# A hybrid attention, convolution and expert layer on one core: u blocks between the queries, pacing by VectorE time, gate writes on another queue, and attention values in column halves

## The chip, the cores and the metric

The kernel runs on one core of a Trainium2 chip. The metric is the device time of one execution in microseconds; less is better. Before the change the median of three runs was 1781.04 us (1773.59 to 1781.09).

The engines go by short names in the profile: PE is TensorE (matrix products; PEld is its loading of weights), DVE is VectorE, ACT is ScalarE, POOL is GpSimd, and SP is SyncE, which only issues transfers. SPq and ACTq are the instruction queues of SyncE and ScalarE where they issue a transfer or wait.

## The reference

One layer of a streaming encoder over 512 tokens of width 1024, in float32. What matters here:

- A projection of the normed input gives queries, keys and values of eight heads, an index branch that selects 128 keys per query, a convolution branch and gates. Attention and convolution are mixed by the gates, projected by w_out, and added to x.
- Then a mixture of 16,384 single-neuron experts. Each token has eight heads; each head scores 128 row keys and 128 column keys, takes the 16 best of both, and the 16 best of their sums. That selects 128 experts per token, with a softmax gate per head. In the reference:

```
u = expert_u[et]
v = expert_v[et]
act = jax.nn.gelu(jnp.einsum('tnd,td->tn', u, xt)) * gt
return jnp.einsum('tn,tnd->td', act, v)
```

- A last gated embedding closes the layer.

## The kernel before, in words

The tokens lie in four tiles of 128. The four tiles' experts are worked out in two different ways.

**Tile 0, gathered.** For its 128 tokens the selected rows of peer_u and peer_v are fetched one expert slot at a time by an indirect transfer (line 799), 128 for u and 128 for v. For each, VectorE runs one operation over 128 x 1024 elements (a dot product, L812, or a weighted sum, L814). With eight Gelu steps this makes 264 steps of the generator `gathered` (L777). `tick` (L827) takes `us / TICK` steps of it; the constants QTICK, RTICK, WTICK, RATE_UV and RATE_V say how many are taken in each phase.

**Tiles 1 to 3, dense.** For these 384 tokens all 16,384 experts are computed, in 128 blocks of 128 experts. A u block (`u_prep` L959, `u_step` L968) loads 128 x 1024 of u (`ut`), splits it into a high part `uh` (ScalarE, L964) and a remainder `ul` (VectorE, L965), multiplies (24 matmuls of 128 x 384, L972 to L974) into a PSUM bank `tp` and applies Gelu on ScalarE into `sg` (L975). There are two `tp` banks. A v block multiplies the gated result with 128 rows of v (L1055 to L1061).

The gates of the dense part must stand in a table G_d in DRAM, by expert block and token, before the first v block. They are made by `gates_dense` (L904), tile by tile: `select` (L704) finds the 16 best of the candidate sums and their expert numbers on VectorE, with two small operations on ScalarE (an Exp, L732, and a copy, L744); three transposes on TensorE (L910) turn the result; then, for each of four parts of 32 tokens, one-hot matrices `ohj`, `ohi` and products `og` are made on VectorE (L930 to L933, 128 x 2048 elements each), TensorE multiplies them (`scatter` L942, L948 and L949), ScalarE copies to `stg` (L951), and ScalarE's queue issues four writes of 512 KB to G_d (L956) when a part is complete.

**The phases.** The order is as follows. The times are rough, read from the trace.

1. Up to about 300 us: input projections, index, convolution and attention for tile 0's queries (`attention` L583, `softmax` L536, `weigh` L562).
2. 300 to 400: attention of tiles 1 to 3 is worked in behind `branches`, `residual` and `query` of tile 0.
3. 400 to 500: `branches` (L619) and `residual` (L641) of tiles 1 to 3. Between the four products of `branches`, steps of `sel0` (the selection for tile 0) are taken.
4. 500 to 590: `query` (L833) of tiles 1 to 3. Each of four rounds multiplies by 512 columns of w_peer_q (`prod_T`, with splits `whi` L161 and `wlo` L162), copies the result (`qT`, L839), and runs `rank` (L689) on each tile: scores on TensorE (L692) and, on VectorE, the 16 best of each of four key sets.
5. 590 to 940: the loop of WARM = 64 u blocks (L990). With it runs the generator `work`: all of `gates_dense`, 58 steps. WPACE = 0.9 steps are taken per block, whatever their length. Each pair of u blocks writes its `sg` to DRAM.
6. 940 to 1440: 64 rounds, each with a u block and a v block, and gather steps at RATE_UV.
7. To the end: the v blocks of the first 64, gather steps at RATE_V, and the closing embedding.

**What sets the order.** The Python code says what depends on what. Within an engine the framework puts instructions in an order planned beforehand: earlier lines of the program come first where their operands are expected to be there, later ones fill in. `tc.high_priority()` moves instructions ahead (each u block's preparation two blocks ahead, for instance); `tc.issue_after` keeps one behind another. At run time every engine takes its instructions strictly in that order. A tile pool with `bufs=n` gives n buffers; whoever takes the next one waits for the last reader of that buffer.

Of the kernel before, what the change touches and what calls it, by code (L numbers as in the profile page):

```python
# [34 lines left out]
WPACE = 0.9  # L35
WTICK = 0.5
QTICK = 25.0
# [5 lines left out]
RATE_UV = 0.36  # L43
RATE_V = 0.147
# [24 lines left out]
def layer_kernel(ctx: ExitStack, tc: tile.TileContext, a, out):  # L69
# [31 lines left out]
    def f(t):  # L101
        return t.bitcast(F32)
# [10 lines left out]
    class Stream:  # L113
# [19 lines left out]
        def nat_T(self, pieces, K, x):  # L133
            M = sum(p[2] for p in pieces) // P
            ps = [mm()[:, :x.shape[-1]] for _ in range(M)]
# [426 lines left out]
    def weigh(ap_, top, qt, pr_, L):  # L562
# [11 lines left out]
        av = tp()[:, :2 * P]  # L574
        for kt in range(nk):
            pe.matmul(av, V[:, kt, pr_ * P:(pr_ + 1) * P], PT[:, kt].rearrange("p s q -> p (s q)"),
                      start=(kt == 0), stop=(kt == nk - 1))
# [126 lines left out]
    def select(t, gate, i_out, j_out):  # L704
# [17 lines left out]
        for h in range(H):  # L722
# [9 lines left out]
        act.activation(ex, ex, AF.Exp)  # L732
        sm = sl_.tile([P, H], F32, name="exs", bufs=1)
        v.tensor_reduce(out=sm, in_=ex, axis=AX, op=ALU.add)
        v.reciprocal(sm, sm)
        v.tensor_tensor(out=gate.rearrange("p (k h) -> p h k", h=H), in0=ex,
                        in1=sm.unsqueeze(2).to_broadcast([P, H, 16]), op=ALU.mult)
# [6 lines left out]
        act.activation(dl[:, 0:3:2, 0], sT[:, :, 0], AF.Copy)  # L744
        v.tensor_sub(dl[:, 0:3:2, 1:16], sT[:, :, 1:16], sT[:, :, 0:15])
        mk = sl_.tile([P, 16, P], F16, name="mk", bufs=1)
# [12 lines left out]
        yield  # L759
# [5 lines left out]
        yield  # L765
# [67 lines left out]
    def query(pl, x, xlo, ts, tick=None):  # L833
        for n in range(4):
# [46 lines left out]
    with lpool("y0") as yp:  # L881
        m0 = yp.tile([P, DC, TD], F32R, name="m0")
        m1 = yp.tile([P, DC, TD], F32R, name="m1")
        with lpool("y1") as y1:
            branches(y1, P, TD, m0, m1, lambda us: next(first, None))
        for _ in first:
            pass
        es_0.close()
        with lpool("y2") as y2:
            residual(y2, (1, 2, 3), m0, m1, None, h2_hi, h2_lo, tick, ple)  # L890
    with lpool("qp") as qp:
        query(qp, h2_hi, h2_lo, (1, 2, 3), tick)
# [3 lines left out]

    es_d = ExitStack()
    up = es_d.enter_context(tc.tile_pool(name="up", bufs=1, side="right", reuse_waits="tile"))
# [5 lines left out]
    def gates_dense(t):  # L904
        tt = t - 1
        ijg = gb.tile([P, 3, P], F32, name="ijg", bufs=1)
        yield from select(t, ijg[:, 2], ijg[:, 0], ijg[:, 1])
        p = mm()
# [8 lines left out]
        for part in range(4):  # L917
            stg = gb.tile([P, P // 4, 32, 4], F32, name="stg", bufs=2)
            for t0 in (0, 8):
# [14 lines left out]
                for q0 in (0, 4):  # L934
# [3 lines left out]
                    yield  # L938
# [3 lines left out]
    def scatter(tt, part, t0, q0, stg, ohj, og):  # L942
# [10 lines left out]
        if t0 + q0 == 12:  # L953
            c0 = tt * P + 32 * part
            for b0 in range(0, P // 4, 8):
                act.dma_start(out=G_d[b0:b0 + 8, :, c0:c0 + 32, :].rearrange("b j t f -> j b (t f)"),  # L956
                              in_=stg[:, b0:b0 + 8].rearrange("p b t f -> p b (t f)"))

    def u_prep(i):  # L959
        ut = up.tile([P, DC, P], F32, name="ut", bufs=UTB)  # L960
        sp.dma_start(out=ut, in_=a["uT"][i])
        uh = up.tile([P, DC, P], F32R, name="uh", bufs=UD + 1)
        ul = up.tile([P, DC, P], F32R, name="ul", bufs=UD + 1)
        act.activation(uh, ut, AF.Copy)  # L964
        anchor[0] = v.tensor_sub(ul, ut, f(uh)).ins  # L965
        return uh, ul

    def u_step(uh, ul, sg, s):  # L968
        p = tp()[:, :TD]
        for c in range(DC):  # L970
            xh, xl = h2_hi[:, c, :], h2_lo[:, c, :]
            pe.matmul(p, uh[:, c, :], xh, start=(c == 0), stop=False)  # L972
# [264 lines left out]
```

## Time and profile before

| What | Value |
|---|---|
| Runs | 1781.04, 1781.09, 1773.59 us |
| The profiled execution's own time | 1776.63 us |
| Its span | 1774.9 us |
| ScalarE, GpSimd busy | 661 us, 427 us |
| Transfers | 441.74 MB, 249 GB/s on average |
| G_d writes | 48 of 512 KB, ScalarE's queue |
| Loads of ut and vt | 128 each of 512 KB, SyncE's queue |

How to read the lines of the profile. A group line gives the line of code, engine, operation, what is written and read, shapes and count; then busy time and the mean of one in ns; then the idle time of the engine just before, and what ended it. A wait line says which engine waited at which line for which instruction: total, times, longest. A timeline line begins with the start time and the duration, and ends in brackets with the idle time before it. A line of stretches gives the length, then the busy time of each engine, then the share of TensorE's clock that was granted, the busy share of the transfer engines, and GB/s. Matmuls overlap in the pipeline, and the profile models their ends, so what one costs is read from the distance of two starts. A float32 matmul appears as two records.

### The profile page before, as it was taken

To read this page: it belongs to the slowest core of one execution; us is meant where nothing else is said; L and a number is where in the kernel's file an instruction comes from. 1 tells how busy PE (TensorE), PEld (TensorE's weight loads), DVE (VectorE), ACT (ScalarE), POOL (GpSimd) and SP (SyncE) were. 2 spreads that over 40 slices of the span, in tenths; PEclk is the share of its full clock that TensorE was granted. 3 is DMA by queue.
4 is the path that set the end of the run, shared out by engine and by line. 5 is a ranking of instruction groups with operands and counts; after the bars stand their busy time and mean duration, and the time that the engine had idled before them with its cause. 6 is when DMAs were issued, how large, how long until landed. Compare 5 with 4: busy or idle time off the path is not lost.

```text
span 1774.9 us, 24360 instructions
## 1 busy us (share of the span) xinstructions
PE 1717.2 (97%) x9033; PEld 1487.6 (84%) x9033; DVE 1362.3 (77%) x2489; ACT 660.9 (37%) x981; POOL 427.5 (24%) x301
## 2 busy tenths in 40 slices
PE   6999999999999899999999999999999999999998
PEld 5777677586788888999999999999999988888887
DVE  4889779648769999996857878877877857667763
ACT  3233343340353244444444333333333333334431
POOL 0021000211112113120113645445545511111100
PEclk9999999999999999999999999999999999999999
DMA  5432325756875468788899999899989878888921
GB/s 163 145 120 84 100 84 184 255 174 192 293 266 155 129 227 280 236 273 260 288 293 378 391 329 337 321 340 330 353 306 344 308 260 311 311 291 314 376 87 69
DMA packets 189815, 441.74 MB, mean 249 GB/s; under 512 B 15192, under 2 KB 76888, under 8 KB 189440
## 3 DMA queue, kind: packets, MB, share of 16 engines
q1 hardware_dynamic: 100528, 273.72, 45.1%
q0 software_dynamic: 36864, 134.23, 21.4%
q10 hardware_dynamic: 52304, 32.24, 6.1%
q8 instruction: 71, 1.16, 0.3%
q14 instruction: 48, 0.39, 0.1%
HBM read 391.86 MB, written 52.46 MB: 250 GB/s over the span
## 4 chain that ended last, share of the span: by engine, by line
PE 59%; DVE 7%; issue 4%; DMA 2%; ACT 1%; POOL 0%; SPq 0%; DVEq 0%; ACTq 0%; POOLq 0%
PE tp L972 9%; PE tp L973 9%; PE tp L974 9%; PE mm L1059 6%; PE mm L1060 6%; PE mm L1061 6%; PE at L1060 3%; PE at L1061 3%; PE at L1059 3%; DMA wr<-in_w_ple_gate_dram 1%; PE mm L948 1%; PE mm L949 1%; DVE ul L965 1%; DVE si L702 1%; DVE sc L699 1%
## 5 line engine op out<-in xcount | busy, mean ns | idle before, releaser
L972 PE MATMUL tp<-h_hi,uh 128*128 128x384 f32 x1024 | 350.9, 343 | 11.5 <-ACT sg L975 11.5
L973 PE MATMUL tp<-h_lo,uh 128*128 128x384 f32 x1024 | 347.7, 340 | 0.0
L974 PE MATMUL tp<-h_hi,ul 128*128 128x384 f32 x1024 | 347.4, 339 | 0.0
L799 POOL DMA_INDIRECT grow<-in_peer_u_dram,eidx x128 | 189.0, 1476 | 480.9 <-DVE grow L812 198.2
L799 POOL DMA_INDIRECT grow<-in_peer_v_dram,eidx x128 | 187.3, 1463 | 398.6 <-DVE grow L812 197.9
L1052 DVE TENSOR_TENSOR vl<-vt,vh 128x1024 fp32r<-128x1024 f32 x128 | 156.4, 1222 | 107.7 <-ACT vh L1051 107.5
L964 ACT ACTIVATE uh<-ut 128x1024 fp32r<-128x1024 f32 x128 | 135.5, 1060 | 277.0 <-PE tp L973 252.8
L965 DVE TENSOR_TENSOR ul<-ut,uh 128x1024 fp32r<-128x1024 f32 x128 | 155.8, 1219 | 79.2 <-ACT uh L964 64.4
L972 PEld LDWEIGHTS tp<-h_hi,uh 128*128 128x128 f32 x1024 | 194.7, 190 | 14.6 <-ACT sg L975 13.4
L1051 ACT ACTIVATE vh<-vt 128x1024 fp32r<-128x1024 f32 x128 | 134.9, 1056 | 185.4 <-PE at L1061 138.1
L1059 PE MATMUL mm<-vh,ah 128*128 128x512 f32 x512 | 200.0, 391 | 0.0
L1060 PE MATMUL mm<-vl,ah 128*128 128x512 f32 x512 | 199.2, 389 | 0.3 <-DVE vl L1052 0.3
L1061 PE MATMUL mm<-vh,al 128*128 128x512 f32 x512 | 199.5, 390 | 0.0
L973 PEld LDWEIGHTS tp<-h_lo,uh 128*128 128x128 f32 x1024 | 194.8, 190 | 1.1
L974 PEld LDWEIGHTS tp<-h_hi,ul 128*128 128x128 f32 x1024 | 194.9, 190 | 0.0
L814 DVE SCALAR_TENSOR_TENSOR acc<-grow,gact,acc 128x1024 f32<-128x1024 f32 x128 | 164.3, 1283 | 0.0
L812 DVE SCALAR_TENSOR_TENSOR grow<-grow,h2row 128x1024 f32<-128x1024 f32 x128 | 155.0, 1215 | 5.0 <-DMA grow<-in_peer_u_dram,eidx 5.0
L161 ACT ACTIVATE whi<-wraw 128x1024 fp32r<-128x1024 f32 (+1 forms) x70 | 71.6, 1022 | 178.9 <-PE mm L176 76.5
L162 DVE TENSOR_TENSOR wlo<-wraw,whi 128x1024 fp32r<-128x1024 f32 (+1 forms) x70 | 82.0, 1174 | 42.8 <-ACT whi L161 38.5
L1061 PEld LDWEIGHTS mm<-vh,al 128*128 128x128 f32 x512 | 96.1, 188 | 20.7
L1060 PEld LDWEIGHTS mm<-vl,ah 128*128 128x128 f32 x512 | 96.1, 188 | 19.6 <-DVE vl L1052 0.7
L1059 PEld LDWEIGHTS mm<-vh,ah 128*128 128x128 f32 x512 | 96.1, 188 | 18.8
(310 smaller groups left out, 3191.5 us busy)
## 6 DMA issues: line engine op xcount, KB each, us to landing
ut<-in_uT_dram SPq DMA_DIRECT2D x128, 512.0 KB
vt<-in_peer_v_dram SPq DMA_DIRECT2D x128, 512.0 KB
G_d<-stg ACTq DMA_DIRECT2D x48, 512.0 KB
gi<-G_d SPq DMA_DIRECT2D x32, 768.0 KB
wraw<-in_w_in_dram SPq DMA_DIRECT2D x32, 512.0 KB
wraw<-in_w_peer_q_dram SPq DMA_DIRECT2D x32, 512.0 KB
sg_d<-sg SPq DMA_DIRECT2D x32, 384.0 KB
sgl<-sg_d SPq DMA_DIRECT2D x32, 384.0 KB
```

Source lines behind the costliest of these rows:

```text
L799: pool.indirect_dma_start(out=r, out_offset=None, in_=a["peer_v" if kind else "peer_u"], in_offset=bass.IndirectOffsetOnAxis(ap=eidx[:, s: ...
L812: v.scalar_tensor_tensor(r, r, 1.0, h2row, op0=ALU.mult, op1=ALU.mult, accum_out=dots[:, s:s + 1])
L814: v.scalar_tensor_tensor(acc, rows.pop(k), gact[:, s:s + 1], acc, op0=ALU.mult, op1=ALU.add)
L964: act.activation(uh, ut, AF.Copy)
L965: anchor[0] = v.tensor_sub(ul, ut, f(uh)).ins
L972: pe.matmul(p, uh[:, c, :], xh, start=(c == 0), stop=False)
L973: pe.matmul(p, uh[:, c, :], xl, start=False, stop=False)
L974: pe.matmul(p, ul[:, c, :], xh, start=False, stop=(c == DC - 1))
L1052: anchor[0] = v.tensor_sub(vl, vt, f(vh)).ins
L1059: pe.matmul(o, xh, vh[:, ks], start=first, stop=False)
L1060: pe.matmul(o, xh, vl[:, ks], start=False, stop=False)
L1061: pe.matmul(o, xl, vh[:, ks], start=False, stop=last)
```

## The change

Six things change together.

1. **u blocks between the queries.** The first EARLY = 8 of the 64 u blocks are moved into `query` of the last tiles: before the first two of the three calls of `rank` in each of the four rounds, one u block is run (`between`, with `u_block`), followed by QU = 0.9 gather steps. The QTICK gather steps after each round are gone. The loop of early u blocks runs from 8 to 63. The pool `up` is opened earlier for that.
2. **Pacing by VectorE time.** The steps of `select` and `gates_dense` now yield a cost in us of VectorE time (6.0, 6.0, 2.6, 5.9, 5.5, 3.0 for a selection, 1.5 + 1.33 x TS for a scatter step), and the loop takes steps as long as a budget lasts that grows by DB = 3.1 per u block. The two halves of the candidate search are separate steps.
3. **Gather steps moved.** WTICK's half step per u block is gone. Instead 1.5 gather steps come after each selection, before the transposes, and TS = 0.42 after each scatter step. RATE_UV goes from 0.36 to 0.38, RATE_V from 0.147 to 0.17.
4. **In `select`,** the copy L744 goes from ScalarE to VectorE; the Exp is issued one step later than its operand is made; the sum, reciprocal and gate product go to the end.
5. **Gate writes by SyncE.** The four G_d writes of a part are issued by SyncE's queue instead of ScalarE's.
6. **Attention values in column halves** (`weigh`), and **other PSUM banks in `branches`**: the second half (n = 1) of each product of the last tiles goes to the banks `at, at, tp, tp`. In `branches` two steps of `sel0` are taken where one was.

The core of the diff:

```
-WPACE = 0.9
-WTICK = 0.5
-QTICK = 25.0
+EARLY = 8
+QU = 0.9
+TS = 0.42
+DB = 3.1
-RATE_UV = 0.36
-RATE_V = 0.147
+RATE_UV = 0.38
+RATE_V = 0.17
...
-        av = tp()[:, :2 * P]
+        av = tp()[:, :P]
         for kt in range(nk):
-            pe.matmul(av, V[:, kt, pr_ * P:(pr_ + 1) * P], PT[:, kt].rearrange("p s q -> p (s q)"),
-                      start=(kt == 0), stop=(kt == nk - 1))
-        for s in range(2):
-            sl = slice(64 * s, 64 * s + 64)
-            act.activation(attT[sl, pr_, qt * P:(qt + 1) * P], av[sl, s * P:(s + 1) * P], AF.Copy)
+            for s in range(2):
+                pe.matmul(av[64 * s:64 * s + 64], V[:, kt, pr_ * P + 64 * s:pr_ * P + 64 * s + 64], PT[:, kt, s],
+                          start=(kt == 0), stop=(kt == nk - 1))
+        act.activation(attT[:, pr_, qt * P:(qt + 1) * P], av, AF.Copy)
...
-                ps = W.nat_T([(w, 512 * n, 512)], 4, x2[:, :, q0:q0 + N])
+                ps = W.nat_T([(w, 512 * n, 512)], 4, x2[:, :, q0:q0 + N],
+                             (at, at, tp, tp) if n and mlo is not None else None)
...
-        act.activation(dl[:, 0:3:2, 0], sT[:, :, 0], AF.Copy)
+        v.tensor_copy(dl[:, 0:3:2, 0], sT[:, :, 0])
         v.tensor_sub(dl[:, 0:3:2, 1:16], sT[:, :, 1:16], sT[:, :, 0:15])
+        yield 2.6
...
         lookup(w, edges[:, 0], 0, 2)
-        yield
+        yield 5.9
+        act.activation(ex, ex, AF.Exp)
...
             for k, t in enumerate(ts):
+                if fill and k < 2:
+                    fill()
                 rank(pl, t, n, qT, k * P)
-            if tick:
-                tick(QTICK)
...
+    def u_block():
+        i = warmed[0]
+        warmed[0] += 1
+        if i == 0:
+            ready.extend(u_prep(k) for k in range(UD))
+        with tc.high_priority():
+            ready.append(u_prep(i + UD))
+        if i % 2 == 0:
+            pair[0] = sg_pair()
+        u_step(*ready.pop(0), pair[0], i % 2)
+        if i % 2:
+            sp.dma_start(out=sg_d[i // 2], in_=pair[0])
+
+    def between():
+        u_block()
+        tick(TICK * QU)
+
     with lpool("qp") as qp:
-        query(qp, h2_hi, h2_lo, (1, 2, 3), tick)
+        query(qp, h2_hi, h2_lo, (1, 2, 3), between)
...
         yield from select(t, ijg[:, 2], ijg[:, 0], ijg[:, 1])
+        tick(TICK * 1.5)
+        yield 3.0
...
                     pend.append(lambda o=(tt, part, t0, q0, stg, ohj, og): scatter(*o))
-                    yield
+                    tick(TICK * TS)
+                    yield 1.5 + 1.33 * TS
...
-                act.dma_start(out=G_d[b0:b0 + 8, :, c0:c0 + 32, :].rearrange("b j t f -> j b (t f)"),
+                sp.dma_start(out=G_d[b0:b0 + 8, :, c0:c0 + 32, :].rearrange("b j t f -> j b (t f)"),
...
-    for i in range(WARM):
-        with tc.high_priority():
-            ready.append(u_prep(i + UD))
-        pace += WPACE
-        while pace >= 1:
-            pace -= 1
-            next(wk, None)
-        tick(TICK * WTICK)
...
+    for i in range(EARLY, WARM):
+        budget += DB
+        while budget > 0:
+            cost = next(wk, None)
+            if cost is None:
+                break
+            budget -= cost
+        u_block()
```

Steps of `work` that are left after the loop are run at its end, before the phase of u and v blocks, as before.

More of the change, by code (lines that the diff above doesn't have):

```diff
@@ L131, in behind, with nat_T @@
                 self.hook(n)
-        def nat_T(self, pieces, K, x):
+        def nat_T(self, pieces, K, x, banks=None):
             M = sum(p[2] for p in pieces) // P
-            ps = [mm()[:, :x.shape[-1]] for _ in range(M)]
+            ps = [(banks[m] if banks else mm)()[:, :x.shape[-1]] for m in range(M)]
             for c0 in range(0, K, 2):
@@ L728, in select @@
             v.max_index(tj[:, h, 8:16], ts[:, h, 8:16], c2)
-        yield
+            if h % 4 == 3:
+                yield 6.0
         ex = sl_.tile([P, H, 16], F32, name="ex", bufs=1)
         v.tensor_tensor(out=ex, in0=ts, in1=ts[:, :, 0:1].to_broadcast([P, H, 16]), op=ALU.subtract)
[L732 to L737, printed above, removed]
         w = sl_.tile([P, P], F16, name="wpos", bufs=1)
@@ L764, in select @@
         add(j_out, md[:, 0, 0], md[:, 0, 1])
-        yield
+        sm = sl_.tile([P, H], F32, name="exs", bufs=1)
+        v.tensor_reduce(out=sm, in_=ex, axis=AX, op=ALU.add)
+        v.reciprocal(sm, sm)
+        v.tensor_tensor(out=gate.rearrange("p (k h) -> p h k", h=H), in0=ex,
+                        in1=sm.unsqueeze(2).to_broadcast([P, H, 16]), op=ALU.mult)
+        yield 5.5
     def sel0():
@@ L831, in tick, with query @@
             next(gt, None)
-    def query(pl, x, xlo, ts, tick=None):
+    def query(pl, x, xlo, ts, fill=None):
         for n in range(4):
@@ L884, in layer_kernel @@
         with lpool("y1") as y1:
-            branches(y1, P, TD, m0, m1, lambda us: next(first, None))
+            branches(y1, P, TD, m0, m1, lambda us: [next(first, None) for _ in range(2)])
         for _ in first:
@@ L890, in layer_kernel, with u_prep, u_step, sg_pair @@
             residual(y2, (1, 2, 3), m0, m1, None, h2_hi, h2_lo, tick, ple)
+    es_d = ExitStack()
+    up = es_d.enter_context(tc.tile_pool(name="up", bufs=1, side="right", reuse_waits="tile"))
+    def u_prep(i):
+        ut = up.tile([P, DC, P], F32, name="ut", bufs=UTB)
+        sp.dma_start(out=ut, in_=a["uT"][i])
+        uh = up.tile([P, DC, P], F32R, name="uh", bufs=UD + 1)
+        ul = up.tile([P, DC, P], F32R, name="ul", bufs=UD + 1)
+        act.activation(uh, ut, AF.Copy)
+        anchor[0] = v.tensor_sub(ul, ut, f(uh)).ins
+        return uh, ul
+    def u_step(uh, ul, sg, s):
+        p = tp()[:, :TD]
+        for c in range(DC):
+            xh, xl = h2_hi[:, c, :], h2_lo[:, c, :]
+            pe.matmul(p, uh[:, c, :], xh, start=(c == 0), stop=False)
+            pe.matmul(p, uh[:, c, :], xl, start=False, stop=False)
+            pe.matmul(p, ul[:, c, :], xh, start=False, stop=(c == DC - 1))
+        act.activation(sg[:, :, s], p, AF.Gelu_apprx_tanh)
+    def sg_pair():
+        return up.tile([P, TD, 2], F32, name="sg", bufs=LEAD // 2 + 2)
+    ready, warmed, pair = [], [0], [None]
+    def u_block():
[13 more added lines that the diff above has]
+        tick(TICK * QU)
     with lpool("qp") as qp:
-        query(qp, h2_hi, h2_lo, (1, 2, 3), tick)
+        query(qp, h2_hi, h2_lo, (1, 2, 3), between)
     es_mid.close()
@@ L895, in layer_kernel @@
     open_sel(es_s)
-    es_d = ExitStack()
-    up = es_d.enter_context(tc.tile_pool(name="up", bufs=1, side="right", reuse_waits="tile"))
     es_g = ExitStack()
```

31 lines of the change are left out of this document (3 added, 28 removed).

## The prediction

> **What bounds the kernel now.** I read the page first, then busy time by stretches, then TensorE's own waits, then single waits in the timelines.
>
> ```profile
> span 1774.9 us, 24360 instructions
> ...
> PE 1717.2 (97%) x9033; PEld 1487.6 (84%) x9033; DVE 1362.3 (77%) x2489; ACT 660.9 (37%) x981; POOL 427.5 (24%) x301
> ```
>
> TensorE is busy for 97% of the span, so only what it stands idle, or runs at a lower clock, can be won. The stretches say where that is:
>
> ```profile
> core 0: us, PE busy (x) PEld busy (x) DVE busy (x) ACT busy (x) POOL busy (x), PEclk, DMA share, GB/s
> 300.00:500.00 200.00, 191.73 (x988) 141.72 (x987) 135.66 (x457) 67.01 (x157) 32.56 (x23) 0.99 0.71 230
> 500.00:950.00 450.00, 427.21 (x2911) 412.57 (x2911) 380.86 (x938) 193.03 (x304) 81.37 (x50) 0.98 0.77 246
> 800.00:900.00 100.00, 100.00 (x734) 97.73 (x734) 73.21 (x71) 44.51 (x73) 10.12 (x10) 1.00 0.87 281
> 1000.00:1400.00 400.00, 400.00 (x2039) 365.51 (x2038) 322.23 (x361) 142.81 (x175) 205.36 (x140) 1.00 0.92 335
> 630.00:634.00 4.00, 4.00 (x16) 4.00 (x15) 4.00 (x7) 0.60 (x2) 0.00 (x0) 0.57 0.66 161
> 937.00:942.00 5.00, 4.63 (x18) 4.63 (x19) 3.51 (x4) 2.59 (x4) 1.08 (x1) 0.66 0.94 248
> ```
>
> From 1000 to 1400 TensorE has no idle time, and nothing can be won there. From 500 to 950, the queries of the last three tiles and the 64 early u blocks, it is idle for 450 − 427.2 = 22.8 us, and the clock was 0.98. That loss of clock sits in five short stretches, of which the first and the last stand above (the others begin near 685, 726 and 770): 0.43 × 4 = 1.7 us and 0.34 × 5 = 1.7 us, so some 8.6 us in five. VectorE is the busiest other engine there, 381 of 450 us. The waits of TensorE in that stretch, in total, times, longest:
>
> ```profile
> PE tp L972 <- ACT sg L975: 11.5, 6, 2.9
> PE mm L177 <- DVE wlo L162: 5.2, 6, 1.3
> PE mm L910 <- DVE ijg L711: 2.1, 1, 2.1
> PE mm L948 <- ACT stg L951: 1.7, 2, 1.5
> PE tp L692 <- ACT qT L839: 1.7, 1, 1.7
> PE tp L692 <- ACT scr L694: 0.5, 1, 0.5
> ```
>
> They sum to 22.7 us, all of the idle time. Half is a u block that waits for a PSUM bank, which ScalarE's Gelu (sg) has not emptied. ScalarE is busy 193 of 450 us; it is late because it runs in order and stands still behind something else. Two examples from its timeline:
>
> ```profile
> 620.33 0.21 ACT L744 ACTIVATE dl<-sT 128x16 f16<-128x16 f16 x1 [8.30 <-DVE sT L741]
> ```
>
> ```profile
> 928.57 8.20 ACTq L956 DMA_DIRECT2D G_d<-stg  x4
> 936.81 0.51 ACT L975 ACTIVATE sg<-tp 128x384 f32<-128x384 f32 x1 [8.27 <-DMA G_d<-stg]
> ```
>
> The first is a copy in the selection that waited 8.3 us for VectorE, with the Gelu queued behind it. The second is the issue of four gate writes, 8.2 us of ScalarE's queue.
>
> **The change, part by part.** All sums are against the profiled execution, 1776.63 us (span 1774.9 and 1.7 around it). It lies within the three timed runs (1773.59 to 1781.09), 4.4 us under their median.
>
> ScalarE's queue. The dl copy becomes VectorE's (three, 0.21 us each by the row above, nothing beside 381). The Exp moves one step of the selection later, its sum and reciprocal to the end, and the transposes come after 1.5 gather steps, so that ScalarE and TensorE find their operands ready. The gate writes leave ScalarE for SyncE. That takes the causes of 11.5 (sg), 2.1 (ijg) and 1.7 (stg): −15.3 us. In the queries, a u block now stands between a query's last product and its first scores and hides the copy of qT: −2.2 (qT, scr). The wlo waits remain in kind, because VectorE still ranks there, but the u block gives time to prepare weights; I take half: −2.6. Together −20.1 us.
>
> The clock. The five slow stretches each follow such a stall. With most stalls gone I take four of five: −6.9 us. [...]
>
> Branches. In the second call of branches the column half n = 1 gets four banks of its own instead of those that VectorE still empties:
>
> ```profile
> PE mm L141 <- DVE ymx L629: 3.7, 6, 1.3
> ```
>
> This is TensorE's wait between 300 and 500. Tile 0's call keeps the old banks; I take three quarters: −2.8. The bounds are 0 and 3.7. That the selection's steps now come two at a time there changes nothing: the same work in twice as many pieces.
>
> Column halves (L576). Each matmul of 256 columns, half of whose results is thrown away, becomes two of 64 output columns by 128. Nothing before shows column halves; row halves (L550) are the nearest rows:
>
> ```profile
> L576 PE MATMUL tp<-PT,V 128*128 128x256 f32 x80 | 20.3, 384 | 0.4 <-ACT PT L572 0.4
> ```
>
> ```profile
> 338.57 1.02 PE L152 MATMUL mm<-wraw,m 128*128 128x512 f32 x2
> 339.43 1.46 PE L576 MATMUL tp<-PT,V 128*128 128x256 f32 x6
> 340.72 0.59 PE L152 MATMUL mm<-wraw,m 128*128 128x512 f32 x1
> ```
>
> ```profile
> 333.01 1.45 PE L152 MATMUL mm<-wraw,m 128*128 128x512 f32 x3
> 334.39 0.92 PE L550 MATMUL at<-k_T,q_T 64*128 64x384 f32 x4
> 335.23 1.12 PE L152 MATMUL mm<-wraw,m 128*128 128x512 f32 x2
> ```
>
> Six records of L576 take 340.72 − 339.43 = 1.29 us, 0.215 each, 17.2 for 80. A pass of 384 columns should take 0.32; four L550 records took 0.84 in all, so the halves do run side by side (0.64). Going into that form and out again costs the rest: 335.23 less the 334.30 at which L152's successor would have started (333.01 + 1.45 − 0.59 + 0.43) is 0.93, less 0.64, and L152 then takes 1.12 for two where 1.02 is usual: about 0.39 us. Column halves: 8.6 us instead of 17.2, and 16 changes of form (4 tiles × 4 pairs) × 0.39 = 6.2: −2.4. The bounds are +6.2 (one after the other) and −8.6 (changes free). I take −2.4, because L550 is measured in the same place. One copy instead of two per pair saves time only on ScalarE, which isn't late there.
>
> Pacing. Prices:
>
> ```profile
> L965 DVE TENSOR_TENSOR ul<-ut,uh 128x1024 fp32r<-128x1024 f32 x70 | 85.2, 1218 | 52.8 <-ACT uh L964 38.0 <-DMA G_d<-stg 10.8 <-PE mm L949 3.9
> L933 DVE TENSOR_TENSOR og<-ohi,ggT 128x2048 f16<-128x2048 f16 x48 | 56.7, 1215 | 0.1
> L812 DVE SCALAR_TENSOR_TENSOR grow<-grow,h2row 128x1024 f32<-128x1024 f32 x29 | 34.8, 1217 | 5.0 <-DMA grow<-in_peer_u_dram,eidx 5.0
> ```
>
> ```profile
> 600.14 0.34 PE L972 MATMUL tp<-h_hi,uh 128*128 128x384 f32 x1
> ...
> 604.30 0.34 PE L972 MATMUL tp<-h_hi,uh 128*128 128x384 f32 x1
> ```
>
> ```profile
> L972 PE MATMUL tp<-h_hi,uh 128*128 128x384 f32 x164 | 56.4, 344 | 0.0
> ...
> L948 PE MATMUL mm<-og,ohj 128*128 128x128 f16 x120 | 15.5, 220 | 0.0
> ```
>
> A u block is 24 matmuls, eight of them of L972: 604.30 − 600.14 = 4.16 us. The last two rows are of 800 to 900: 164/8 = 20.5 blocks and 120/8 = 15 scatter steps fill 100 us of TensorE, so a step takes (100 − 20.5 × 4.16)/15 = 0.98. On VectorE two steps share four operations of 1.22 us, 2.43 a step; a block takes 1.22, a gather step 1.22. Gather steps before: 4 × 25/7 in the queries, 64 × 0.5 in the loop: 46.3. After: 8 × 0.9 + 3 × 1.5 + 48 × 0.42 = 31.9. So 14.4 steps, 17.6 us of VectorE, leave the stretch for the later phases: demand 381 − 18 = 363 against 450 − 31 = 419 us of TensorE's work. Within the scatter stretches the budget of 3.1 buys 3.1/(1.5 + 1.33 × 0.42) = 1.51 steps a block: VectorE 1.22 + 1.51 × 2.43 + 0.63 × 1.22 = 5.65, TensorE 4.16 + 1.51 × 0.98 = 5.64. That is a draw, covered by the selections, whose charge (29 a tile) leaves VectorE room: I take 0, bounds 0 and +9 (5% on 32 blocks). In the phase of 1000 to 1400, ten more steps cost VectorE 12 us over some 480, at 322 of 400 busy: nothing. DMA, at 0.92 there, gets ten times 128 rows of 4 KB more, 5 MB, 10 GB/s on 335: nothing.
>
> The end of the loop. The charges sum to 3 × 29 + 48 × 2.06 = 186, the loop spends 56 × 3.1 = 174: six scatter steps are left after the last block. They need 6 × (2.43 + 0.51) = 17.6 us of VectorE; TensorE has their 5.9 us and two prepared blocks, 8.3. The stall is 3.4, with one slow-clock stretch (1.7) +5.1; bounds 0 (later u blocks cover it) and +11.6 (another 8.2 of gate writes stand bare, in place of the clock).
>
> Gate writes on SyncE. Behind them now queue the loads of ut, the writes of sg and, at the end, gi and vt:
>
> ```profile
> 906.86 0.33 SPq L961 DMA_DIRECT2D ut<-in_uT_dram  x1
> ```
>
> ```profile
> 919.98 1.06 ACT L964 ACTIVATE uh<-ut 128x1024 fp32r<-128x1024 f32 x1 [1.38 <-PE tp L973]
> ```
>
> Three ut buffers, one refilled every block: this load was issued 13.1 us before its use, and its weights are made two blocks (8.3) ahead of TensorE. Cover 21 us against a hold of 8.2: I take 0.
>
> Sum: −20.1 − 6.9 − 2.8 − 2.4 + 5.1 = −27.1, that is 1749.5; I say 1750.
>
> **Rivals.** *VectorE takes over.* For: 381 of 450 today, and the order of its work is planned beforehand; behind each wait for sg stand selection and scatter operations, with ul queued after them, so that the u block may wait for ul instead. Against: 363 of 419 after the change. If half of the idle time and clock comes back (13.5) and the scatter stretches cost their 9, it is 1750 + 22.5: 1772.
>
> *Halves one after the other.* For: no row shows column halves. Against: row halves do run side by side. −2.4 becomes +6.2: 1758.
>
> *It doesn't do what it says.* The planner may leave the u blocks behind the queries, if VectorE's work stands ahead of their weights. The queries' 2.2 and 2.6 aren't won then: 1755.
>
> *SyncE's queue becomes the bound (slower).* Its rows:
>
> ```profile
> G_d<-stg ACTq DMA_DIRECT2D x48, 512.0 KB
> ```
>
> Four make one group, 2 MB, 12 groups. A write waits for the last copy of its part, and ut loads wait behind it in the queue, then behind its data. It decides when hold and write together exceed the 21 us of cover; a miss of 3.4 us with 1.7 of slow clock at each of 12 groups is 61 us: 1811. For: the last group held its queue 8.2 us. Against: that must more than double. [...]
>
> **How the numbers follow.** Chances: forecast 0.68, VectorE 0.12, halves 0.09, u blocks not moved 0.06, SyncE 0.05. About 0.5%, 8.9 us, is what can be told from no change; against the profiled execution that is 1767.7. The forecast's own bounds: all idle time and clock won, branches 3.7, halves −8.6, gives 1776.6 − 43.7 = 1733; on the other side 1750 + 9 (scatter) + 6.5 (end of the loop) is 1765. The runs scatter by 4 either way, so the range goes from 1729 to 1771; SyncE's case and half of VectorE's lie outside. Faster: 0.66 + 0.03 + 0.08 + 0.06 = 0.83; the same: 0.02 + 0.08 + 0.01 = 0.11; slower: VectorE 0.01, SyncE 0.05 = 0.06.
>
> **What would show it.** Right: TensorE's wait of tp on sg falls from 11.5 to under 3; the stretch of queries and early u blocks holds at most one or two slow-clock stretches and under 10 us idle; no ScalarE wait names G_d; ymx falls under 1; L576's 160 records start in pairs a few ns apart. Wrong: uh waits on ut by more than 1 us in many places; VectorE at 100% with TensorE waiting for ul or og; a stall of 8 us or more before the first v matmul; L576 records one after another.

## The result and the profile after

The changed kernel takes **1765.07 us** (median of six runs, 1759.25 to 1768.46) against 1776.85 for the kernel before (six runs beside it): ratio **0.9923, interval 0.9907 to 0.9940**. The profiled execution is the fastest of the six, 1759.25 us, 17.4 us under the profiled one of before (1776.63). One of the six executions of the last experiment (e12) took 9652.83 us, the others 1757 to 1769; it is left out of that kernel's ratio.

The page of the changed kernel, the lines that answer to those of before:

```profile
span 1757.5 us, 24524 instructions
...
PE 1707.3 (97%) x9113; PEld 1479.0 (84%) x9113; DVE 1361.3 (77%) x2493; ACT 655.6 (37%) x961; POOL 463.0 (26%) x301
```

Busy time by stretches, changed kernel (columns as in the prediction). The first two answer to stretches shown of before; the last two hold its slow-clock stretches:

```profile
500.00:950.00 450.00, 434.54 (x2962) 419.86 (x2962) 378.10 (x934) 198.61 (x305) 105.33 (x42) 0.98 0.75 242
1000.00:1400.00 400.00, 400.00 (x2034) 365.35 (x2033) 329.97 (x372) 142.81 (x175) 219.90 (x148) 1.00 0.94 343
649.00:654.00 5.00, 4.79 (x19) 4.80 (x20) 5.00 (x32) 0.55 (x2) 0.34 (x1) 0.66 0.74 262
929.00:944.00 15.00, 10.88 (x29) 9.09 (x30) 12.00 (x14) 7.49 (x9) 3.05 (x2) 0.54 0.91 355
```

From 500 to 950 TensorE is idle for 450 − 434.5 = 15.5 us instead of 22.8. The clock is 0.98 as before. There are two slow stretches instead of five, but the second is long: 0.34 × 5 = 1.7 us of clock were withheld in the first, 0.46 × 15 = 6.9 in the second. Not all of that is lost time, because TensorE was idle for 4.1 of these 15 us. The second stretch itself lasts 13.65 us, from 929.65 to 943.30, of which TensorE was idle for 3.5; the other 10.2 us went at a granted clock of 0.50, so by the clock 5.1 us were lost. That makes 6.8 us in all, against 8.6 before. From 1000 to 1400 TensorE is full as before; the gather steps moved there cost VectorE some 8 us of 400 and nothing else.

TensorE's waits from 500 to 950, changed kernel (total, times, longest):

```profile
PE tp L910 <- ACT sg L913: 8.4, 4, 6.2
PE mm L955 <- DVE ijg L712: 3.2, 1, 3.2
PE mm L1078 <- ACT vh L1070: 1.6, 1, 1.6
PE mm L994 <- DVE og L978: 1.4, 2, 1.0
PE tp L693 <- ACT sg L913: 0.5, 1, 0.5
PE mm L994 <- ACT stg L997: 0.4, 2, 0.2
```

The waits of the queries (wlo, qT, scr: 7.4 us before) are gone. What is new stands mostly at one place, the end of the loop: 6.2 us for sg and 1.6 for vh, next to each other. ScalarE's timeline shows why sg was late:

```profile
917.78 0.49 ACT L913 ACTIVATE sg<-tp 128x384 f32<-128x384 f32 x1
929.96 1.06 ACT L902 ACTIVATE uh<-ut 128x1024 fp32r<-128x1024 f32 x1 [11.69 <-DMA ut<-in_uT_dram]
930.92 0.50 ACT L913 ACTIVATE sg<-tp 128x384 f32<-128x384 f32 x1
```

and SyncE's why that ut was:

```profile
909.15 13.89 SPq L1002 DMA_DIRECT2D G_d<-stg  x4
923.13 2.94 SPq L899 DMA_DIRECT2D ut<-in_uT_dram  x2
927.28 0.80 SPq L1039 DMA_DIRECT2D gi<-G_d  x2
```

The last group of gate writes held SyncE's queue for 13.9 us. The ut load behind them was issued at 923.13, its split uh began at 929.96, and the Gelu stood behind uh on ScalarE.

Behind the same writes lies a second path, the pieces of the changed kernel's chain of work ahead of the first v block (start, us, what):

```profile
912.11 15.09 DMA G_d<-stg
927.28 4.15 DMA gi<-G_d
...
934.08 0.83 ACT ah L1061
...
936.29 1.00 ACT vh L1070
937.33 2.08 PE mm L1078 x4
```

The third write landed 15 us after its issue; only then could the gates be read (gi), multiplied and split (ah). So two things could be the cause: the queue that the writes hold, or the way of the gates through DRAM. In the changed kernel's last group the four issues took 0.4, 2.5, 7.7 and 3.1 us.

### The profile page after: what moved, and what is told of

Read it like the earlier page. It is cut to its first block, busy times and chain, and to the rows that moved or that the text cites. A ratio compares the mean times of both kernels' runs of the same rounds, so it can differ in the third digit from the quotient of the medians.

```text
span 1757.5 us, 24524 instructions
## 1 busy us (share of the span) xinstructions
PE 1707.3 (97%) x9113; PEld 1479.0 (84%) x9113; DVE 1361.3 (77%) x2493; ACT 655.6 (37%) x961; POOL 463.0 (26%) x301
## 4 chain that ended last, share of the span: by engine, by line
PE 66%; DVE 5%; DMA 2%; issue 1%; ACT 1%; SPq 0%; DVEq 0%; ACTq 0%
PE tp L910 9%; PE tp L911 8%; PE tp L912 8%; PE mm L1079 7%; PE mm L1078 7%; PE mm L1080 7%; PE at L1078 3%; PE at L1079 3%; PE at L1080 3%; PE mm L177 1%; PE mm L178 1%; PE mm L176 1%; DVE ul L903 1%; PE mm L994 1%; PE mm L995 1%; DMA G_d<-stg 1%
## 5 line engine op out<-in xcount | busy, mean ns | idle before, releaser
L802 POOL DMA_INDIRECT grow<-in_peer_u_dram,eidx x128 | 215.2, 1681 | 485.3 <-DVE grow L815 252.3
L802 POOL DMA_INDIRECT grow<-in_peer_v_dram,eidx x128 | 196.1, 1532 | 347.3 <-DVE grow L815 169.5
L910 PEld LDWEIGHTS tp<-h_hi,uh 128*128 128x128 f32 x1024 | 193.5, 189 | 11.6 <-ACT sg L913 10.4
L815 DVE SCALAR_TENSOR_TENSOR grow<-grow,h2row 128x1024 f32<-128x1024 f32 x128 | 155.4, 1215 | 2.0 <-DMA grow<-in_peer_u_dram,eidx 2.0
L1080 PEld LDWEIGHTS mm<-vh,al 128*128 128x128 f32 x512 | 96.7, 189 | 20.1
```

Source lines behind the costliest of these rows:

```text
L802: pool.indirect_dma_start(out=r, out_offset=None, in_=a["peer_v" if kind else "peer_u"], in_offset=bass.IndirectOffsetOnAxis(ap=eidx[:, s: ...
L815: v.scalar_tensor_tensor(r, r, 1.0, h2row, op0=ALU.mult, op1=ALU.mult, accum_out=dots[:, s:s + 1])
L1080: pe.matmul(o, xl, vh[:, ks], start=False, stop=last)
```

## The experiments

Ratios are against the kernel before, run beside each. "Chain" is the distance from the start of the last scatter matmul to that of the first v matmul. It is 926.9 to 955.7 = 28.8 us in the kernel before and 907.3 to 937.3 = 30.0 after.

**1. The last group on ScalarE's queue** (e1).

```
-sp.dma_start(out=G_d[...
+(act if tt == 2 and part == 3 else sp).dma_start(out=G_d[...
```

> The changed kernel, with only the last of the twelve groups of gate writes (tile 3, part 3) put back on ScalarE's queue. In the changed kernel TensorE stands idle for 6.2 and 1.6 us at the end of the loop of early u blocks, and its clock is at half for 13.7 us after that: some 14.5 us. Theory A (SyncE's queue): the last group held SyncE's queue from 909.1 to 923.0 and the ut load behind it came late. Then the wait of uh on ut (11.7 us) goes, and what comes back is the hold of ScalarE as before the change, about 1.9 us idle and 1.7 of clock: 10 to 11 us less than the changed kernel, 0.986 of the kernel before. Theory B (six scatter steps left over keep VectorE busy): the stall stays, the time is that of the changed kernel, 0.992.

Measured: 1768.99 us, 0.9951 (0.9935 to 0.9967). SyncE's queue was free of the last group, and the stall grew. Timeline of ScalarE's queue, then TensorE's longest wait, then SyncE's, all of this kernel:

```profile
916.37 14.74 ACTq L1002 DMA_DIRECT2D G_d<-stg  x4
```

```profile
PE tp L910 <- ACT sg L913: 13.2, 4, 11.0
```

```profile
SPq L1039 <- DMA G_d<-stg: 17.2, 1, 17.2
```

The hold moved to ScalarE, where the Gelus stand behind it. The chain stayed (30.6 us). The longer stall cost no more, because more of the slow stretch fell into it: idle time and lost clock at the end of the loop are 11.0 + 1.6 = 12.6 us here and 7.8 + 5.1 = 12.9 in the changed kernel. The third row is the important one: with its queue free, SyncE itself stood still for 17.2 us at the read of the gates until the writes had landed, with the next ut and vt loads behind it.

**2. All gate writes on ScalarE's queue** (e2): one part of the change undone.

```
-sp.dma_start(out=G_d[...
+act.dma_start(out=G_d[...
```

> The changed kernel with all gate writes back on ScalarE's queue. Theory A: the stall at the loop's end shrinks as in the run with the last group alone (-10 to -11 us against the changed kernel), but inside the loop the u blocks wait again for Gelus behind the issue of gate writes: before the change some 5 us of idle time and two stretches of slow clock, +8. So about 0.990 to 0.992 of the kernel before, and the wait of tp on sg above 5 us within the loop. Theory B: no gain at the end, only the +8: 0.996.

Measured: 1768.36 us, 0.9941 (0.9919 to 0.9963), 0.0018 above the changed kernel, about 3 us, which the intervals don't separate. TensorE's idle time from 500 to 960 was 460 − 443.2 = 16.8 us (15.5 after): pieces of up to 4 us in several places instead of one. At the end of the loop it stood idle for 4.5 us, and the chain was 23.4 us: the write that the chain waits for landed 10.1 us after its issue, where it took 15.1 in the changed kernel.

**3. A larger budget** (e3), so that no scatter step is left over at the end of the loop.

```
-DB = 3.1
+DB = 3.6
```

> The changed kernel with DB = 3.6 instead of 3.1, so that all gate steps fit into 52 of the 56 blocks and none are left over. Theory B (left-over steps): the stall at the loop's end vanishes, -12 us, 0.985 of the kernel before. Theory A: the last two groups of writes follow each other as closely as before and hold SyncE's queue four blocks earlier, where the ut loads stand behind them just the same; the stall moves to an earlier place and stays, and VectorE, now charged 17% more per block, brings its own waits: the changed kernel's time or up to 6 us more, 0.992 to 0.995.

Measured: 1764.62 us, 0.9902 (0.9871 to 0.9932). The last scatter came at 891.0, among the u blocks, and the first v block 51.8 us later. TensorE's waits from 500 to 960:

```profile
PE tp L910 <- ACT sg L913: 4.5, 4, 3.3
PE mm L955 <- DVE ijg L712: 4.2, 1, 4.2
PE mm L994 <- DVE og L978: 3.3, 1, 3.3
```

The stall at the end fell to 3.3 us, though the last group held SyncE for 12.0 us here too. In exchange TensorE now waits for VectorE inside the loop (ijg, og: 7.5 us instead of 4.6), each with a slow-clock stretch behind it (the clock from 500 to 950 was 0.99).

**4. Two writes on each queue** (e4).

```
-sp.dma_start(out=G_d[...
+(act if b0 % 16 else sp).dma_start(out=G_d[...
```

> The changed kernel with each group's four gate writes taken in turn by SyncE's and ScalarE's queues, two each. In both traces the first two issues of a group take 0.4 and 0.6 us, the third and fourth 1 to 8 us, since the queue takes no more until the first have drained. Theory A, with that room counted for each queue by itself: each queue is held for 1 us a group, no ut load and no Gelu is late, and both the stall at the end (14.5 us) and the in-loop waits stay away: -12 us against the changed kernel, 0.985 of the kernel before. If the room is shared by both queues or the transfer engines themselves are full, both queues are held for several us and nothing is won: 0.990 to 0.994. Theory B: the changed kernel's time.

Measured: 1767.6 us, 0.9939 (0.9920 to 0.9958). The holds are short now, 1.7 us on ScalarE and 3.3 on SyncE, and the stall is still there, ahead of 939.5. Waits of TensorE from 500 to 960 and of SyncE, this kernel:

```profile
PE mm L1078 <- ACT vh L1070: 11.4, 1, 11.4
```

```profile
SPq L1039 <- DMA G_d<-stg: 16.2, 1, 16.2
```

This settles the first question: the hold of the issuing queue is not the cause. Idle time and lost clock at the end are 11.9 + 2.0 = 13.9 us, no less than with the long hold. The order in a queue still matters a little: the last link of e4's chain is a vt load that stood behind the read of the gates (issued at 931.76, vh at 938.38), though ah ran only from 936.24, so an earlier vt could have gained some 2 us. The chain is 29.4 us, as in the other kernels with these left-over steps and four blocks ahead (30.0, 30.6 in e1, 29.6 in e8), but for e2 (23.4): the write that it waits for needs 15.1 us from issue to landing in the changed kernel and 19.0 in e4, and gi, ah and vh or vt the rest. What differs from before is how many u blocks TensorE has meanwhile. Before, the last scatter came behind u block 64 and the first v block behind 70, six blocks. After the change 4.75 blocks stand between them, in e1 and e4 4.25.

**5. Six u blocks ahead of the v blocks instead of four** (e5).

```
-LEAD = 4
+LEAD = 6
...
-name="sg", bufs=LEAD // 2 + 2
+name="sg", bufs=LEAD // 2 + 1
```

> The changed kernel with LEAD = 6 instead of 4 (and as many sg buffers as before, four): one more pair of u blocks is computed ahead of the first v block. Theory C (cover): from the last scatter to the first v block some 29 us pass in every trace so far, in the kernel before (28.8), the changed one (30.0), with the last group on ScalarE's queue (30.6) and with both queues in turn (29.4), because the gate writes must land before the gates are read back; what counts is how many u blocks lie in between, six before the change and 4.7 after it. Two more blocks are 8.3 us of work, so the idle time at the first v block (7.8 to 11.4 us) falls to under 3 us and the half-clock stretch after it to one of 3.4 us: -10 us against the changed kernel, 0.986 of the kernel before. Theory A (the held queue makes ut late): the two blocks more need ut loads that stand behind the same writes, and the stall stays: 0.992.

Measured: **1758.99 us, 0.9902 (0.9881 to 0.9922)**. Idle time from 500 to 960 fell from 15.5 to 460 − 448.6 = 11.4 us, and the end of the loop from 7.8 us to 3.8, with one slow-clock stretch of 3.4 us in place of 13.65. It was less than the expected cure: 3.8 us is left. It is a wait for a PSUM bank, and ScalarE's timeline shows the Gelu that empties it behind the first v block's two ah, which waited for the gates:

```profile
939.25 1.77 ACT L1061 ACTIVATE ah<-sg 128x768 fp32r<-128x768 f32 x2 [6.05 <-issue]
940.93 0.50 ACT L913 ACTIVATE sg<-tp 128x384 f32<-128x384 f32 x1
```

**6. Only the gate writes on SyncE** (e6), all else as before.

```
-act.dma_start(out=G_d[...
+sp.dma_start(out=G_d[...
```

> The kernel before with nothing changed but the gate writes, which SyncE issues instead of ScalarE. Their part in the prediction: of the 11.5 us of waits of tp on sg, the four inside the loop that follow gate writes (some 5 us with stg's 1.7) and two stretches of slow clock (3.4) go, and the one at the loop's end (1.9 and 1.7) with six blocks of cover; -8 to -12 us, 0.994. Rival (the queue's choice hardly matters, as the runs with the changed kernel suggest, where all writes on ScalarE cost 0 to 4 us): 0.997 to 1.0.

Measured: 1771.7 us, 0.9965 (0.9950 to 0.9980): 6 us, between the expectation (0.994) and its rival (0.997 to 1.0). With six u blocks behind the last scatter the end of the loop has one wait of 1.7 us.

**7. No u block between the queries** (e7).

```
-EARLY = 8
+EARLY = 0
...
-        query(qp, h2_hi, h2_lo, (1, 2, 3), between)
+        query(qp, h2_hi, h2_lo, (1, 2, 3), lambda: tick(TICK * QU))
```

> The changed kernel without u blocks between the queries (EARLY = 0; the 0.9 gather steps at each of the eight places stay), so that all 64 run in the loop and the budget of 3.1 lasts for all gate steps with 12 us to spare: the gate steps end four blocks before the loop does. If the u blocks between the queries are what counts, the queries' waits (7.5 us of wlo, qT and scr) come back and the time is 4 to 7 us above the changed kernel's. But by theory C the longer cover at the loop's end saves up to 12 us. Both together: 0.988 to 0.993 of the kernel before, with the queries' idle time near 7 us and the first v block's near 0.

Measured: 1763.9 us, 0.9929 (0.9906 to 0.9952), the same as the changed kernel. TensorE's waits from 500 to 960:

```profile
PE tp L910 <- ACT sg L913: 7.6, 3, 2.5
...
PE mm L178 <- DVE wlo L163: 2.3, 4, 1.0
...
PE tp L693 <- ACT qT L842: 0.7, 1, 0.7
```

The queries wait again (2.3 and 0.7, not the 7.4 of before), but with 64 blocks in the loop the budget suffices, the last scatter comes at 886.2, and no wait is left at the end of the loop but one of 2.5 us at 918. What the u blocks gain between the queries they lose as cover: eight blocks of the loop fewer are 8 × 3.1 = 25 us less budget.

**8. Without the column halves** (e8): `weigh` as before.

```
-                pe.matmul(av[64 * s:64 * s + 64], V[:, kt, pr_ * P + 64 * s:...
+            pe.matmul(av, V[:, kt, pr_ * P:(pr_ + 1) * P], PT[:, kt]...
```

> The changed kernel with the attention values as before, one matmul of 256 columns. By the traces, six records of 0.215 us (1.29 us) became twelve that start in pairs 6 ns apart, with a change of form there and back: 1.00 us for three key tiles. Over 4 tiles that is 2 to 3 us, the prediction's 2.4: the time is 2 to 3 us above the changed kernel's, 0.994. Rival: the halves' gain is lost to VectorE's softmax there, and the time is the same, 0.992.

Measured: 1769.52 us, 0.9944 (0.9922 to 0.9967). Against the changed kernel that is 0.0021, 3.7 us, with intervals that overlap. In the profiles TensorE's busy time up to the first u block, less what the half clock added to it, is 482.8 us here and 477.9 in the changed kernel: 4.9 us.

**9. Six blocks ahead and two writes on each queue** (e9): the edits of e4 and e5.

> Six u blocks instead of four ahead of the v blocks, and the gate writes shared, two on ScalarE's queue and two on SyncE's. With six ahead alone, TensorE still stood idle for 3.8 us ahead of the first v block, for a u block whose ut load stood behind the gate writes in SyncE's queue. Theory (cover and queue add up): with the short holds of two and two that idle falls under 1 us and no slow-clock stretch is left there, so the time is 4 to 6 us under that of six ahead alone, ratio to before about 0.987 to 0.988. Rival (the wait is for the split of u on ScalarE or VectorE, not for the load): idle stays at 3 us or more, the time is the same within 2 us.

Measured: 1766.22 us, 0.9926 (0.9899 to 0.9953): a miss, not better than e5; the intervals overlap. SyncE's and ScalarE's timelines of this kernel:

```profile
911.50 3.04 SPq L1002 DMA_DIRECT2D G_d<-stg  x2
930.74 0.81 SPq L1039 DMA_DIRECT2D gi<-G_d  x2
931.65 0.37 SPq L899 DMA_DIRECT2D ut<-in_uT_dram  x1
```

```profile
936.08 0.91 ACT L1061 ACTIVATE ah<-sg 128x768 fp32r<-128x768 f32 x1 [14.75 <-DVE sg L1057]
936.89 0.50 ACT L913 ACTIVATE sg<-tp 128x384 f32<-128x384 f32 x1
```

After the writes SyncE does nothing for 16 us: it stands at the read of the gates, which waits for their landing. ScalarE stands for 14.75 us at ah, which waits for the gates, and the Gelu of a u block that TensorE finished long before stands behind it. TensorE waits 9.1 us. More u blocks ahead don't help when what they need stands behind the gates in two queues. The wait left in e5 was not for a ut load, as the expectation had it, but for the Gelu shown there. In e5 the two ut loads went out at 925.97, right behind the writes, whose hold ended at 925.87, and ahead of the read at 929.27.

**10. Eight gld buffers in `branches`** (e10), with six blocks ahead.

```
-                    g = pl.tile([P, N], F32, name="gld", bufs=4)
+                    g = pl.tile([P, N], F32, name="gld", bufs=8)
```

It asks where the gain in `branches` went. Stretches of `branches` and of the residual's products, before and after:

```profile
410.00:450.00 40.00, 37.10 (x113) 20.84 (x112) 34.09 (x143) 2.48 (x6) 3.04 (x3) 1.00 0.67 222
450.00:480.00 30.00, 29.54 (x123) 22.68 (x122) 24.31 (x34) 13.76 (x17) 3.56 (x3) 1.00 0.86 280
```

```profile
404.00:444.00 40.00, 40.00 (x126) 23.60 (x125) 35.83 (x149) 4.07 (x7) 3.26 (x3) 1.00 0.68 229
444.00:474.00 30.00, 27.23 (x116) 21.18 (x115) 24.00 (x33) 12.30 (x15) 3.72 (x3) 1.00 0.79 274
```

`branches` itself lost all its idle time, 2.9 us; the residual behind it gained 2.3.

> Six u blocks ahead, and eight instead of four gld buffers in branches. Theory (the gain of the other PSUM banks in branches was given back because loads of w_out stand in SyncE's queue behind gld loads that wait for VectorE): the waits of TensorE in the residual's products for wlo and whi, 2.8 us after the change, fall under 1, the time from the last product of branches to the first of the queries falls from 50.7 to about 48 us, and the whole by 2 to 3 us against six ahead alone. Rival (VectorE itself is late with wlo, being busy with the selection's steps that come two at a time): the waits stay at 2.5 us or more and the stage at 50 to 51 us.

Measured: 1761.85 us, 0.9899 (0.9873 to 0.9925), not told apart from e5. From the last product of `branches` to the first of the queries it is 50.2 us (50.7 after the change, 48.0 before), and the waits for wlo and whi are 2.0 us (2.8 after the change): the theory falls. SyncE's wait at the weight loads there, this kernel (the changed kernel has the same line to the digit):

```profile
SPq L124 <- DVE wlo L163: 17.1, 7, 5.2
```

The w_out loads don't wait for gld. They wait for a wraw buffer that VectorE has not yet split (wlo); VectorE is busy for 36 of 40 us in `branches`. In the kernel before that wait is 16.7 us too, but in nine pieces of at most 2.5: the loads come as late, the products that need them come sooner. That VectorE's work is the limit there is argued from these rows; no run took work from it.

**11. Three edits alone** (e11): before, with gate writes by SyncE, column halves and six blocks ahead.

> The kernel before with three edits alone: gate writes by SyncE, attention values in column halves, six u blocks ahead of the v blocks. No pacing by VectorE time, no u blocks between the queries, no change in the selection or in branches. Theory (the gain of the whole change is the gate writes and the halves; pacing and moving u blocks pay for themselves only): within 3 us of the whole change with six ahead, ratio 0.989 to 0.992. Rival (pacing, selection and u blocks between the queries earn the 6.9 us that the prediction gave them with their share of the clock): 6 us or more above it, ratio 0.993 to 0.996.

Measured: 1771.27 us, 0.9960 (0.9945 to 0.9976), 10 us above e5 (0.0058), whose interval is apart. The theory falls, the rival holds: pacing, the moved gather steps, the edits in `select`, the u blocks between the queries and `branches` together do earn some 10 us. TensorE's waits from 500 to 960:

```profile
PE tp L971 <- ACT sg L974: 9.7, 3, 3.9
PE mm L177 <- DVE wlo L162: 5.6, 7, 1.8
```

20.2 us of idle time, 11.4 in e5: the queries' 7.8 us are back (5.6 for wlo, 1.7 for qT, 0.5 for scr), and in the loop two waits for a Gelu of 2.9 us each stand near 622 and 629, as in the kernel before.

**12. No u block between the queries and six ahead** (e12): the edits of e5 and e7.

> The changed kernel with six u blocks ahead of the v blocks and none between the queries. Without u blocks between the queries the end of the loop had only 2.7 us of idle time even with four ahead, because the last scatter then came earlier among the u blocks. Theory (the u blocks between the queries gain some 5 us there and cost about as much at the end, where cover is then short): with six ahead the end needs no cover, so leaving them out costs 3 to 5 us against six ahead with them, ratio about 0.992 to 0.993. Rival (they gain nothing in the queries): the same within 2 us, 0.989 to 0.991.

Measured: 1763.1 us, 0.9913 (0.9883 to 0.9943). The time lies between theory and rival, and the interval holds both. In the profiles TensorE's idle time from 500 to 960 is 460 − 447.8 = 12.2 us, 11.4 with the u blocks there. Whether they earn anything by themselves stays open; at most a few us.

Of the kernels tried, e5 is the fastest by its median. Its lead of 0.0021 on the changed kernel is within the intervals, and by ratio e3, e5 and e10 lie together (0.9902, 0.9902, 0.9899).

## Why the prediction was right, and where it was not

1750 was predicted, within 1729 to 1771, faster with 0.83. 1765 lies in the range, on its upper side. The likeliest case came in kind, except for one term, but not in size: 27.1 us were forecast and 11.8 came by the medians, 17.4 by the profiled executions. That the time lies in the range owes something to the width of the range; the forecast's own bad side, 1750 + 9 + 6.5 with 4 of scatter, is 1769.5, and the range went to 1771. Term by term, in the profiled executions, counted as the prediction counts: the old stall and the old slow stretch at the end of the loop stand in the first two rows, the whole new ones in the row of the end.

| Term | Predicted | Measured |
|---|---|---|
| ScalarE's queue and the queries (idle time 500 to 950, 22.8 to 7.7 without the new end) | −20.1 | −15.1 |
| Clock, the five stretches of before | −6.9 (four of five) | −6.8 (one left) |
| Branches | −2.8 | −0.6 |
| Column halves | −2.4 | −4.4 |
| VectorE's pacing | 0 (0 to +9) | within the first two rows |
| End of the loop | +5.1 (0 to +11.6) | +12.9 |
| SyncE's queue elsewhere | 0 | 0 |
| Sum | −27.1 | −14.0 of −17.4 |

By the prediction's own signs it is half right. What it named came for the number of slow stretches (two), for ScalarE's waits (none names G_d) and for the halves; ymx fell to 1.0, its bound. But TensorE's wait on sg fell to 8.4 and not under 3, and the idle time to 15.5 and not under 10; both miss by what stands at the end of the loop (2.2 and 7.7 without it). Of the signs for wrong, the stall of 8 us ahead of the first v matmul was all but reached (7.8).

**End of the loop: the term that failed.** It is 7.8 us of idle time and 5.1 of lost clock, 12.9, where 3.4 + 1.7 was taken and +11.6 was the bound. Against the 1.9 and 1.7 that stood there before, the end got 9.3 us longer. The prediction counted six left-over steps; in the trace seven scatter steps follow the 64th u block, two before the change, and they are the trigger: e3, which leaves none, shrinks the stall to 3.3. But it priced them as VectorE's work. VectorE's timeline is empty there from 919 to 931. What the steps do is put off the last gate writes against the u blocks, and then the gates' way through DRAM (15 us to land, 4 to be read, 6 until the first v matmul) lies bare. The prediction's upper bound, gate writes that stand bare, was nearest, and it named the wrong cover: two prepared u blocks, where it takes all of those whose ut loads are issued ahead of the gates' read. In the traces it is the issuing queue that waits for the landing: SyncE stood 16.2 and 17.2 us at gi in e4 and e1, and ut and vt loads followed directly.

**SyncE's queue.** The rival with 12 misses of 5 us (1811) did not come: in the changed kernel's loop, ahead of its end, ScalarE's uh never waited for a ut load, as the cover of 21 us had it. The last group of writes held the queue 13.9 us where 8.2 was taken. A ut load that followed those writes was usable 6.8 us after its issue (923.13 to 929.96), and the median of all is 6.2:

```profile
ut<-in_uT_dram SPq DMA_DIRECT2D x128, 512.0 KB, 6.2
...
G_d<-stg SPq DMA_DIRECT2D x48, 512.0 KB, 6.7
```

It did land behind the data of the writes (929.9, the fourth write 928.6; all 549 landings of SyncE's queue that the changed kernel's trace shows stand in the order of their issue), but hardly later than the median load. Late was its issue.

**ScalarE's queue.** The sg waits ahead of the end fell from 9.6 to 2.2 us, stg from 1.7 to 0.4, the queries' 7.4 to 0.5, better than the half of wlo that was taken. What is left of sg in the loop stands behind the Exp, which found its operand late although it was moved a step (ScalarE's timeline, changed kernel, ahead of the wait at 742):

```profile
738.85 0.31 ACT L757 ACTIVATE ex<-ex 128x128 f32<-128x128 f32 x1 [3.93 <-DVE ex L733]
```

What failed is ijg: −2.1 was counted, and the wait grew to 3.2, with og 1.4 new. These are VectorE's. Its timeline ahead of the wait shows the moved gather steps (L815) standing in front of the selection's last operation:

```profile
644.63 1.22 DVE L815 SCALAR_TENSOR_TENSOR grow<-grow,h2row 128x1024 f32<-128x1024 f32 x1
...
646.11 1.27 DVE L815 SCALAR_TENSOR_TENSOR grow<-grow,h2row 128x1024 f32<-128x1024 f32 x1
...
648.88 0.28 DVE L712 TENSOR_TENSOR ijg<-md 128x128 f32<-128x128 f16 x1
```

The 1.5 gather steps were to give ScalarE and TensorE time ahead of the transposes; in the planned order they came ahead of what the transposes wait for. This is read from the order; no run took them away alone. The pacing's bounds (0 to +9) hold: 2.5 us more wait for ijg and og, and the one slow stretch left (1.7).

**Clock.** Three of the four stretches ahead of the end are gone, and a long one came at the end. At a granted clock of 0.50 the five of before and the first one after lasted 3.41 us each, the long one 13.65, four times as long. The long one began 4.4 us into the stall of 6.2 us and covered the stall of 1.6 us that came 4 us behind it, and cost 5.1 us besides them. The prediction took one stretch (1.7) there.

**Branches.** −2.9 in `branches`, +2.3 in the residual: the prediction named no successor for that stall, and there was one.

**Column halves.** They run side by side. TensorE's timeline, changed kernel:

```profile
336.22 0.82 PE L571 MATMUL tp<-ident,L 128*128 128x128 f32 x6
336.87 1.88 PE L153 MATMUL mm<-wraw,m 128*128 128x512 f32 x4
338.68 0.88 PE L578 MATMUL tp<-PT,V 128*64 128x128 f32 x12
339.49 1.98 PE L153 MATMUL mm<-wraw,m 128*128 128x512 f32 x4
```

Twelve records, two for every half of three key tiles, go by in 0.81 us (338.68 to 339.49). One after the other they would take 1.3, by the six records of 128 columns of L571 (336.22 to 336.87, 0.108 each). By the prediction's way: L153's successor would have started at 338.59 (336.87 + 1.88 − 0.59 + 0.43) and started at 339.49, 0.90 later, and four of it then took 1.98 where 1.88 is usual, so 1.00 us where 1.29 was paid before. Less 0.39 for the changes of form, 0.61 for six old records, 8.1 for 80, and with 16 changes 14.3 instead of 17.2: −2.9. Measured as a whole it is more. Up to the first u block e11 differs from before in the halves alone; TensorE's busy time there, less what the half clock added, is 543.4 us against 547.8: −4.4. The 4.9 of e8 is near it, and the 3.7 by its ratio fits both. By that sum the 16 changes of form cost 17.2 − 4.4 − 8.1 = 4.7 us, some 0.3 each instead of 0.39; this is an estimate.

Of the 17.4 us, 3.4 are in no term: 1.7 is a slow stretch near 357 that came and went between runs of the same code there (the clock from 300 to 500 was 0.99 before, 1.00 after and 0.99 again in e5), 1.2 lies ahead of 300, and 0.5 I can't assign. The profiled execution is the fastest of its six; by the medians the gain is 11.8.

**Still open.** Why the write that the chain waits for needs 15.1 us to land, and 19.0 in e4, where the median is 6.7. The share of the transfer engines was high there (changed kernel):

```profile
920.00:925.00 5.00, 5.00 (x31) 4.95 (x29) 0.00 (x0) 0.00 (x0) 0.00 (x0) 1.00 1.11 365
```

The share alone can't be the reason: in e5 it was 1.06 to 1.13 from 915 to 930, and the write landed 9.1 us after its issue. No run took other transfers away, so the cause is not shown. Nor was a read of the gates tried from a queue that nothing else stands in.

## What to carry to other kernels

When a table goes through DRAM between two phases, cost its whole way (issue, landing, read back, first use) and count what work is *already fed* behind the last write; moving the last writes to another queue only moved who stood still here (ScalarE for 14.7 us in e1, where SyncE had stood for 13.9). The read that waited for a write to land stopped its whole queue for 16 to 17 us (e1, e4, e9), so loads for the covering work should be issued ahead of it. And when work is moved forward to fill one gap, look at what it covered where it stood: here the u blocks filled the queries and were missed at the end of the loop.

## What the runs showed of the hardware that was not expected

- Of four 512 KB gate writes in a row, the first was issued in 0.4 us; the whole last group held the queue 8.2 (before), 13.9 (after) and 14.7 us (e1), on ScalarE as on SyncE. In the changed kernel, e1 and e5 the fourth issue ended within 0.2 us of the landing of the first write (923.0 and 922.9; 931.1 and 931.1; 925.9 and 925.9); in all twelve groups of the changed kernel it ended 0.0 to 2.9 us after that landing, in none ahead of it. Two on each queue held them 1.7 and 3.3 us only.
- A stall of TensorE of 3.2 us, up to 649.2, was followed by 3.4 us at half clock (0.50 from 649.76 to 653.17). In the stall of 6.2 us the half clock began 4.4 us after its start, in that of 11.4 us (e4) 2.2 us after its start, and lasted 13.65 us both times. Not every stall brings it: before the change one of 2.9 us at 619.0 was followed by none, the next of 2.9 us at 626.4 by 3.4 us.
- The two column halves of a pair start 7 ns apart in the records.
